# A trunk layer on one core: q, k and the probabilities of seven head pairs turned by VectorE's 32x32 transposes and a trip through DRAM, the normalization on ScalarE

## The chip, the cores and the metric

The kernel runs on one NeuronCore of a Trainium2 chip. A core has five engines with instruction streams of their own: TensorE (PE; its weight loads are a row of their own, PEld), VectorE (DVE), ScalarE (ACT), GpSimd (POOL) and SyncE (SP), which here does nothing but issue DMAs. Each engine works through its own instructions in the order in which the program lists them and stops at an instruction whose input is not there yet. Data moves between DRAM and the on-chip memory SBUF by DMA, over 16 engines that all queues share. The metric is the device time of one execution in microseconds (us), the median of several runs.

## What is computed

One layer of a diffusion backbone on 128 context tokens and 256 latent tokens with 2048 channels: modulation of the inputs, RMS norm, one input projection into q, k, v (16 heads of 64) and a Fourier branch, attention, gates, output projection, then a SwiGLU network. What the change touches is the attention, cut here to its core:

```
q = rms_norm(q.reshape(shp), q_g)
k = rms_norm(k.reshape(shp), k_g)
...
s_loc = jnp.einsum('brnqhd,brnkhd->bhrnqk', qg, kb).astype(jnp.float32) * scale + bias
s_ctx = jnp.einsum('brnqhd,blhd->bhrnql', qg, k_ctx).astype(jnp.float32) * scale
p = jax.nn.softmax(jnp.concatenate([s_loc, s_ctx], axis=-1), axis=-1).astype(v.dtype)
o = (jnp.einsum('bhrnqk,brnkhd->brnqhd', p[..., :nk], vb)
     + jnp.einsum('bhrnql,blhd->brnqhd', p[..., nk:], v_ctx))
```

Context tokens attend to context tokens only; latent tokens to a window of latent tokens and to the 128 cached context keys. `rms_norm` divides by the root of the mean square and multiplies by a gain. All in float32; the large products are made from three passes over halves of split operands (high times high, low times high, high times low).

## The kernel before

**Stages.** In order: the opening (modulation, first products), the input projection `w_in` (`unit`, from L163, with accumulation into SBUF at L783), the gate projection `w_gate` (the loop over `fc8`, 8 output chunks of 8 weight units), the branch projections `w_fn` and `w_na`, the output projection, the feed-forward part. TensorE's weights always come in units of 512 KB: `load_unit` (L230) issues the load on SP's queue, `split` (L155 on ACT, L156 on DVE) makes the high half `wh` and the low half `wl`, and `unit` multiplies: L170 and L171 with `wh`, L176 with `wl`, 18 products for two rows of weights and the three token tiles.

**Ticks.** The order of the work beside the products is written out by hand. `next_unit` (L249) and `mid_unit` (L245) call the generators in the lists `front` and `behind`; in the gate stage the list `front` holds the branch work (`br_work`: first the Fourier branch, then attention) and the row sums (`rows`), and each of the 64 units ticks them three times: at its start, after the split of a coming unit, and in its middle. So a tick of the gate stage is a third of a unit. `RATES[1]` = 0.62 is how many steps `rows` makes per tick there.

**Row sums.** `mod_rows` (L363 on DVE) multiplies 512 KB tiles of modulation weights by a scalar and adds them up, one instruction of 128x1024 per step; `CHUNKS` gives its steps per unit in the last pass of `w_in`, chunk by chunk in the order 6, 7, 0, 1, 2, 3, 4, 5, and `RATES[2]` in the branch projections. Its result is later added up across partitions by DMAs of the POOL queue. In the last pass of `w_in` a chunk takes five units.

**After a chunk of q or k.** `after` (L734) writes the chunk to DRAM (`s_qkvu`), squares it on ACT, sums per head and takes the inverse root on DVE; for k it also multiplies (L756) before it writes.

**Attention, one head pair at a time.** `attention_pair` (L946) goes through the ticks of the string `PAIR`, separated by commas; two letters name a step, a digit the half (0: the first 128 latent queries and the context queries, 1: the other 128 latent queries):

```
PAIR = "t1 qk,,,,,lq,s0 s1 m0,e0,m1,i0 pv lb,e1,,i1 t0,,lv"
```

`lq`, `lb`, `lv` issue the loads of the next pair (q and k, bias, v). `qk` (`turned`, L956) turns q and k, 128x128 blocks at a time, on TensorE against an identity (L960, L963: six transposes a pair) and copies them out of PSUM with ACT, which applies the gains (L965, L967, L968). `s` makes scores (L977, evicted at L989 to L998 into `sc`, 128 x 2 x 896), `m` the row maxima (L1004, L1008), `e` the exponentials with their sums (L1016, ACT), `i` the reciprocal (L1024) and the multiplication by it (L1026, both DVE: two 128x384 and, for half 0, two 128x128 as well). `t` (`keys_first`, L1028) turns the probabilities on TensorE (L1039: eight 128x128 blocks for half 0, six for half 1) and ACT copies them from PSUM into `pt` (L1041). `pv` multiplies by v (L1056) and evicts (L1060). `t1` and `pv` of a pair run in the ticks of the next one (`rest`); those of the last pair run after the loop.

The kernel already turns two other tensors with VectorE and DRAM, in `mixed` and in `turn_act`: L1142 or L1421 transposes every 32x32 block on DVE, L1146 or L1354 writes the tile to DRAM, and four DMAs (L1149 or L1358) read it back, 32 partitions each, so that the blocks come to their places.

Of the kernel before, what the change touches and what calls it, by code (L numbers as in the profile page):

```python
# [13 lines left out]
F32 = mybir.dt.float32  # L14
F32R = mybir.dt.float32r
AF = mybir.ActivationFunctionType
# [3 lines left out]
P = 128  # L20
# [7 lines left out]
CTX = 128  # L28
# [91 lines left out]
def trunk_kernel(ctx: ExitStack, tc: tile.TileContext, io: dict):  # L120
# [29 lines left out]
    def nm(s):  # L150
        return f"{s}{next(ids)}"
# [134 lines left out]
    s_sum = dram.tile([P, 4 * CH], F32, tag="sum", name="s_sum")  # L286
    s_turn = dram.tile([P, 4, TOK], F32, tag="turn", name="s_turn")

    first = consts.tile([P, 96], F32, tag="first", name="first")
# [17 lines left out]
    with ExitStack() as ph:  # L307
# [6 lines left out]
        def at_tile():  # L314
            return pa.tile([P, CH], F32, tag="at", name=nm("at"))
# [151 lines left out]
        with ExitStack() as pha:  # L467
# [266 lines left out]
            def after(ci):  # L734
                a = acc[ci]
                yield
                if not 2 <= ci < 4:
                    nc.sync.dma_start(s_qkvu[ci], a)
                if 4 <= ci < 6:
                    nc.sync.dma_start(new_v[:, (ci - 4) * CH : (ci - 3) * CH], a[:, 0])  # L740
                if ci >= 4:
                    return
                sq = c6([P, NT, CH], "sq")
                nc.scalar.activation(out=sq, in_=a, func=AF.Square)
                yield
                ss = small.tile([P, NT, 8], F32, tag="ssqk", name=nm("ssqk"))
                nc.vector.tensor_reduce(
                    out=ss, in_=sq.rearrange("p t (h d) -> p t h d", d=HD), axis=AX.X, op=ALU.add
                )
                if ci < 2:  # L750
                    yield from inv_sqrt(rq[:, :, ci * 8 : (ci + 1) * 8], ss, HD, [P, NT, 8])
                else:
# [5 lines left out]
                    nc.sync.dma_start(s_qkvu[ci], a)  # L758
# [147 lines left out]
        def attention():  # L906
            br = ph.enter_context(tc.tile_pool(name="branch", bufs=1))
            for i in range(8):
                aT[i] = br.tile([P, TOK], F32, tag=f"aT{i}", name=f"aT{i}")
            with ExitStack() as st:  # L910
                wk = st.enter_context(tc.tile_pool(name="awk", bufs=1))
                rest = {}
                for hp in range(8):
                    rest = yield from attention_pair(hp, wk, rest)
                rest["t1"]()
                for _ in range(5):
                    yield
                rest["pv"]()
# [5 lines left out]
        def load_qk(hp):  # L924
            ci, co = hp // 4, (hp % 4) * P
            qp = ald.tile([P, NT, P], F32, tag="qp", name=nm("qp"))
            kp = ald.tile([P, 4, P], F32, tag="kp", name=nm("kp"))
# [3 lines left out]
            return qp, kp  # L931

# [13 lines left out]
        def attention_pair(hp, wk, rest):  # L946
            (_, (qp, kp)), (_, bp), (_, vp) = qks[0].take(), biases[0].take(), vs[0].take()
            t = {}
# [7 lines left out]
            def turned():  # L956

                pq = at_tile()
                for i in range(NT):
                    nc.tensor.transpose(pq[:, i * P : (i + 1) * P], qp[:, i], ident)  # L960
                pk = at_tile()
                for i in range(NT):
                    nc.tensor.transpose(pk[:, i * P : (i + 1) * P], kp[:, i], ident)  # L963
                q = t["q"] = wk.tile([P, TOK], F32, tag="q", name=nm("q"))
                nc.scalar.activation(out=q, in_=pq[:, :TOK], func=AF.Identity, scale=qg8)  # L965
                k = t["k"] = wk.tile([P, 4 * P], F32, tag="k", name=nm("k"))
                nc.scalar.activation(out=k[:, :TOK], in_=pk[:, :TOK], func=AF.Identity, scale=qg[:, 1:2])  # L967
                nc.scalar.copy(k[:, TOK:], kp[:, 3])  # L968

# [51 lines left out]
            def inverses(qt):  # L1021
                sm = t["sm", qt]
                n = len(halves[qt])
                nc.vector.reciprocal(sm[:, :n], sm[:, :n])  # L1024
                for i, (j, sl) in enumerate(halves[qt]):
                    nc.vector.tensor_scalar_mul(sc[:, j, sl], sc[:, j, sl], sm[:, i : i + 1])  # L1026

            def keys_first(qt):  # L1028

                if not qt:  # L1030
                    t["pt"] = wk.tile([P, 16, P], F32, tag="pt", name=nm("pt"))
                blocks = [(j, qt * TOK + kc * P) for kc in range(3) for j in range(2)]
                if not qt:
                    blocks += [(j, 2 * TOK) for j in range(2)]
                for b0 in range(0, len(blocks), 4):
                    some = blocks[b0 : b0 + 4]
                    o = at_tile()
                    for i, (j, c0) in enumerate(some):
                        nc.tensor.transpose(o[:, i * P : (i + 1) * P], sc[:, j, c0 : c0 + P], ident)  # L1039
                    dst = slice(8 * qt + b0, 8 * qt + b0 + len(some))  # L1040
                    nc.scalar.copy(  # L1041
                        t["pt"][:, dst], o[:, : len(some) * P].rearrange("p (b q) -> p b q", q=P)
                    )

            def values():
# [3 lines left out]
                for k in range(4):  # L1049
                    for j in range(2):  # L1050
                        s = slice(j * HD, (j + 1) * HD)
                        out, x = po[s, :CTX], pt[:, 6 + j]
                        if k:
                            out = po[s, CTX:TOK].rearrange("p (t q) -> p t q", t=2)
                            x = pt.rearrange("p (t b) q -> p t b q", t=2)[:, :, 2 * k - 2 + j]
                        nc.tensor.matmul(  # L1056
# [8 lines left out]
                **{f"{n}{j}": functools.partial(f, j) for j in range(2) for n, f in (  # L1065
                    ("s", scores), ("m", maxima), ("e", exps), ("i", inverses), ("t", keys_first))},

                **{n: rest.get(n, lambda: None) for n in ("t1", "pv")},
            }
            for tick in PAIR.split(","):  # L1070
# [5 lines left out]
                yield  # L1076
            return {"t1": functools.partial(keys_first, 1), "pv": values}

# [546 lines left out]
```

## Time and profile before

| what | value |
|---|---|
| median of 3 runs | 2006.34 us (2005.43 to 2008.59) |
| the profiled execution: time | 2005.29 us |
| the profiled execution: span of the instructions | 2003.5 us |
| granted TensorE clock | 1.00 |
| attention's work on the engines | about 412 to 647 us from the span's start |

The page of the profile gives, for each engine, the time in which it ran an instruction ("busy") and its share of the span. The chain of work that ended last is found by going back from the last instruction to whatever released it; engines on that chain set the end, the others have room. A group line gives the line of the kernel, engine, operation, the names written and read, the shapes, the count, then busy time in us and the mean duration of one in ns, then the idle time just ahead of these instructions and what ended it. The view of stretches gives busy time per engine inside chosen bounds, the granted clock, the mean busy share of the 16 DMA engines and GB/s. TensorE's instructions are pipelined: one lasts longer than the distance to the next, so what one costs on the path is read from the chain, not from its duration.

### The profile page before, as it was taken

How to read it: one execution, taken by the hardware profiler on the slowest of the kernel's cores; microseconds unless marked ns; L12 is line 12 of the kernel's file. 1: busy time of each engine (PE TensorE's matmuls, PEld its weight loads, DVE VectorE, ACT ScalarE, POOL GpSimd, SP SyncE). 2: the span in 40 equal slices, each digit the busy share in tenths (PEclk: the TensorE clock that was granted, in tenths of full speed). 3: DMA queues.
4: the chain of work that ended last, by engine and by line, in shares of the span. 5: the costliest groups of instructions: out<-in, count | busy, mean ns of one | idle time of the engine just before them, and what ended most of it. 6: DMA issues, size and time to landing. Idle time of an engine off the chain costs nothing.

```text
span 2003.5 us, 24190 instructions
## 1 busy us (share of the span) xinstructions
PE 1989.5 (99%) x9404; PEld 1628.4 (81%) x9404; DVE 1226.0 (61%) x1493; ACT 718.3 (36%) x1052; POOL 73.9 (4%) x106
## 2 busy tenths in 40 slices
PE   8999999999999999999999999999999999999999
PEld 5767888887777888889988888888888888888887
DVE  6745999879877886776843454554334433434654
ACT  6324332445554443344423322323232233223231
POOL 0000010101010100100001000001000000000000
PEclk9999999999999999999999999999999999999999
DMA  9896898888886898764457464547444544455463
GB/s 347 289 342 206 308 288 312 271 278 283 269 255 216 284 330 264 252 231 131 134 182 200 158 189 164 188 139 211 137 150 129 165 153 131 132 152 174 158 185 104
DMA packets 140658, 425.28 MB, mean 212 GB/s; under 512 B 17856, under 2 KB 39296, under 8 KB 139520
## 3 DMA queue, kind: packets, MB, share of 16 engines
q1 hardware_dynamic: 127344, 400.51, 60.4%
q0 software_dynamic: 9600, 16.88, 3.9%
q10 hardware_dynamic: 3600, 6.34, 0.9%
q8 instruction: 74, 1.21, 0.2%
q14 instruction: 40, 0.33, 0.0%
HBM read 387.50 MB, written 44.63 MB: 216 GB/s over the span
## 4 chain that ended last, share of the span: by engine, by line
PE 95%; DMA 2%; DVE 2%; ACT 1%; issue 1%; SPq 0%; DVEq 0%; ACTq 0%
PE mm L170 19%; PE mm L176 18%; PE mm L171 18%; PE at L170 10%; PE at L171 10%; PE at L176 10%; PE at L436 1%; DMA wm<-in_w_mod 1%; PE at L1039 1%; PE at L977 1%; PE at L1056 1%; DVE wl L156 1%; PE at L1447 1%; PE at L1453 1%; PE mm L1453 1%; PE mm L1447 1%
## 5 line engine op out<-in xcount | busy, mean ns | idle before, releaser
L156 DVE TENSOR_TENSOR wl<-wraw,wh 128x1024 fp32r<-128x1024 f32 (+1 forms) x464 | 553.7, 1202 | 435.1 <-ACT wh L155 251.7
L155 ACT CAST wh<-wraw 128x1024 fp32r<-128x1024 f32 (+1 forms) x464 | 478.5, 1038 | 757.9 <-PE mm L171 454.1
L170 PE MATMUL mm<-wh,hH 128*128 128x512 f32 x1316 | 518.2, 394 | 0.3 <-ACT hH L155 0.3
L171 PE MATMUL mm<-wh,hL 128*128 128x512 f32 x1316 | 513.2, 390 | 0.2
L176 PE MATMUL mm<-wl,hH 128*128 128x512 f32 x1316 | 357.2, 389 | 0.2 <-DVE wl L156 0.2
L363 DVE SCALAR_TENSOR_TENSOR accr<-wmr,csz,accr 128x1024 f32<-128x1024 f32 x240 | 301.6, 1278 | 4.6 <-DMA wmr<-in_w_rows 4.6
L170 PEld LDWEIGHTS mm<-wh,hH 128*128 128x128 f32 x1316 | 247.0, 188 | 65.6 <-issue 12.7
L176 PEld LDWEIGHTS mm<-wl,hH 128*128 128x128 f32 x1316 | 246.9, 188 | 52.2 <-DVE wl L156 0.6
L171 PEld LDWEIGHTS mm<-wh,hL 128*128 128x128 f32 x1316 | 247.2, 188 | 50.6 <-DVE hL L156 0.8
L170 PE MATMUL at<-wh,hH 128*128 128x512 f32 x616 | 240.1, 390 | 0.0
L171 PE MATMUL at<-wh,hL 128*128 128x512 f32 x616 | 239.7, 389 | 0.0
L176 PE MATMUL at<-wl,hH 128*128 128x512 f32 x616 | 169.4, 389 | 0.0
L176 PEld LDWEIGHTS at<-wl,hH 128*128 128x128 f32 x616 | 115.6, 188 | 24.0
L171 PEld LDWEIGHTS at<-wh,hL 128*128 128x128 f32 x616 | 115.7, 188 | 23.9
L170 PEld LDWEIGHTS at<-wh,hH 128*128 128x128 f32 x616 | 115.6, 188 | 23.9
L170 PE MATMUL mm<-wh,cH 128*128 128x512 f32 x278 | 108.1, 389 | 0.0
L171 PE MATMUL mm<-wh,cL 128*128 128x512 f32 x278 | 108.1, 389 | 0.0
L176 PE MATMUL mm<-wl,cH 128*128 128x512 f32 x278 | 76.6, 389 | 0.0
L170 PE MATMUL at<-wh,cH 128*128 128x512 f32 x196 | 76.2, 389 | 0.0
L171 PE MATMUL at<-wh,cL 128*128 128x512 f32 x196 | 76.2, 389 | 0.0
L783 DVE TENSOR_TENSOR acc<-acc,mm 128x512 f32<-128x512 f32 x60 | 40.4, 685 | 43.8 <-PE mm L176 43.8
L171 PEld LDWEIGHTS mm<-wh,cL 128*128 128x128 f32 x278 | 52.2, 188 | 10.8
(287 smaller groups left out, 1817.1 us busy)
## 6 DMA issues: line engine op xcount, KB each, us to landing
wraw<-in_w_gate_up SPq DMA_DIRECT2D x176, 512.0 KB, 3.8
wmr<-in_w_rows SPq DMA_DIRECT2D x128, 512.0 KB, 5.2
wraw<-in_w_down SPq DMA_DIRECT2D x88, 512.0 KB, 3.9
wraw<-in_w_gate SPq DMA_DIRECT2D x64, 512.0 KB, 5.0
wraw<-in_w_in SPq DMA_DIRECT2D x60, 512.0 KB, 5.6
wm<-in_w_mod SPq DMA_DIRECT2D x24, 768.0 KB, 6.1
wraw<-in_w_o SPq DMA_DIRECT2D x32, 512.0 KB, 6.2
wm<-in_w_mod SPq DMA_DIRECT2D x28, 512.0 KB, 6.1
```

The source lines that it names most:

```text
L155: nc.scalar.copy(H, x)
L156: nc.vector.tensor_sub(L, x, fr(H))
L170: nc.tensor.matmul(po[t], H[k0 + i][:, sl], wH[:, i], start=first and i == 0, stop=False)
L171: nc.tensor.matmul(po[t], L[k0 + i][:, sl], wH[:, i], start=False, stop=False)
L176: nc.tensor.matmul(po[t], H[k0 + i][:, sl], wL[:, i], start=False, stop=last and i == n - 1)
L363: nc.vector.scalar_tensor_tensor(out=acc[:, cnd], in0=wm, scalar=sc, in1=acc[:, cnd], op0=ALU.mult, op1=ALU.add)
L436: nc.tensor.matmul(pm[q : q + 32, :w], csz[:, k, :], wm[:, kk + par, ty, :], start=k < 2, stop=k >= KT - 2, tile_position=(0, q), skip_gro ...
L783: nc.vector.tensor_add(a, a, po[t])
L977: nc.tensor.matmul(po[j][:, cols], t["q"][rows[j], q], t["k"][rows[j], k], start=True, stop=True, tile_position=(j * HD, 0),)
L1039: nc.tensor.transpose(o[:, i * P : (i + 1) * P], sc[:, j, c0 : c0 + P], ident)
L1447: nc.tensor.matmul(o, a, xH, start=u + kk == 0, stop=False)
L1453: nc.tensor.matmul(o, a, wide(u + kk)[0], start=False, stop=last and kk == 1)
```

## The change

q and k are no longer turned per pair on TensorE. `after` transposes the 32x32 blocks of every chunk of q and k on DVE once, three instructions of 128x512 per chunk (12 in all), and writes the result to new DRAM tiles `s_qk`; the old writes of these four chunks to `s_qkvu` go. `load_qk` reads q and k of a pair from there in four DMAs each, 32 partitions at a time; `turned` is left with three ACT instructions that read SBUF. The new `normed` multiplies the probabilities by their reciprocal sums on ACT instead of DVE, for all eight pairs. For pairs 0 to 6, `block_rows` transposes the 32x32 blocks of `sc` on DVE, `leave` writes them to DRAM (`s_pt`), and `enter` reads them back in four DMAs per half; pair 7 keeps TensorE's transposes. `pt` has a new layout (part, block, 32) that the products read in runs of 32 numbers. `PAIR` puts the new steps in its 15 ticks; `pv` moves two ticks later. The rows' steps per unit in chunks 1, 2, 3 and 4 go down by 0.35 (five units each) and those in the 32 units of the branch projections up by 0.22.

```diff
-PAIR = "t1 qk,,,,,lq,s0 s1 m0,e0,m1,i0 pv lb,e1,,i1 t0,,lv"
+PAIR = "x1 qk,w1,,,r0,lq,s0 s1 m0 r1,e0,m1,v0 lb,n0 e1,v1 pv,n1 x0,w0,lv"
-CHUNKS = [1.95, 1.95, 1.95, 1.6, 1.6, 1.2, 1.2, 1.7]
-RATES = [1.5, 0.62, 1.1, 1.3, 0.452]
+CHUNKS = [1.95, 1.95, 1.95, 1.25, 1.25, 0.85, 0.85, 1.7]
+RATES = [1.5, 0.62, 1.32, 1.3, 0.452]
...
-                if not 2 <= ci < 4:
+                if ci >= 4:
                     nc.sync.dma_start(s_qkvu[ci], a)
...
+                def channels_first():
+                    tr = c6([P, NT, CH], "sq").rearrange("p t n -> p (t n)")
+                    trv = tr.rearrange("p (g k t r) -> p k g t r", g=4, k=4, t=NT)
+                    for t in range(NT):
+                        nc.vector.transpose(
+                            trv[:, :, :, t], a[:, t].rearrange("p (k g r) -> p k g r", k=4, g=4)
+                        )
+                        if t < NT - 1:
+                            yield
+                    yield
+                    nc.sync.dma_start(s_qk[ci], tr.rearrange("p (g k n) -> p g k n", g=4, k=4))
...
-            nc.sync.dma_start(qp, s_qkvu[ci][:, :, co : co + P])
-            nc.sync.dma_start(kp[:, 0:3], s_qkvu[2 + ci][:, :, co : co + P])
-            nc.sync.dma_start(kp[:, 3], io["cache_k"][hp])
+            for x, src in ((qp, s_qk[ci]), (kp, s_qk[2 + ci])):
+                for g in range(4):
+                    nc.sync.dma_start(
+                        x[32 * g : 32 * g + 32], src[:, g, k].rearrange("(a p) n -> p a n", p=32)
+                    )
+            nc.sync.dma_start(kc, io["cache_k"][hp])
...
-                    nc.vector.tensor_scalar_mul(sc[:, j, sl], sc[:, j, sl], sm[:, i : i + 1])
+                    nc.scalar.activation(out=sc[:, j, sl], in_=sc[:, j, sl], func=AF.Copy, scale=sm[:, i : i + 1])
+
+            def block_rows(qt):
+
+                n = 6 if qt else 8
+                tr = t["tr", qt] = wk.tile([P, 4 * 8 * 32], F32, tag="tr", bufs=2, name=nm("ptr"))
+                b = tr[:, : 4 * n * 32].rearrange("p (g b r) -> p b g r", g=4, b=n)
+                for j in range(2):
+                    nc.vector.transpose(
+                        b[:, j:6:2],
+                        sc[:, j, qt * TOK : (qt + 1) * TOK].rearrange("p (c g r) -> p c g r", c=3, g=4),
+                    )
+                if not qt:
+                    nc.vector.transpose(b[:, 6:8], sc[:, :, 2 * TOK :].rearrange("p j (g r) -> p j g r", g=4))
+
+            def leave(qt):
+                n = 6 if qt else 8
+                nc.sync.dma_start(s_pt[qt], t["tr", qt][:, : 4 * n * 32].rearrange("p (g n) -> p g n", g=4))
...
+            def enter(qt):
+
+                if not qt:
+                    new_pt()
+                dst = t["pt"][:, :, 8:] if qt else t["pt"][:, :, :8]
+                for g in range(4):
+                    nc.sync.dma_start(
+                        dst[32 * g : 32 * g + 32].rearrange("p a b r -> p a (b r)"),
+                        s_pt[qt][:, g].rearrange("(a p) n -> p a n", p=32),
+                    )
```

In `PAIR`, `x` is `block_rows` (for pair 7 `keys_first`), `w` is `leave`, `r` is `enter`, `v` the reciprocal and `n` is `normed`; `x1`, `w1`, `r0`, `r1` and `pv` run in the ticks of the next pair.

More of the change, by code (lines that the diff above doesn't have):

```diff
@@ L287, in trunk_kernel @@
     s_turn = dram.tile([P, 4, TOK], F32, tag="turn", name="s_turn")
+    s_pt = [dram.tile([P, 4, n * 32], F32, tag=f"pt{n}", name=f"s_pt{n}") for n in (8, 6)]
+    s_qk = [dram.tile([P, 4, 4, NT * 32], F32, tag=f"sqk{i}", name=f"s_qk{i}") for i in range(4)]
     first = consts.tile([P, 96], F32, tag="first", name="first")
@@ L751, in after @@
                     yield from inv_sqrt(rq[:, :, ci * 8 : (ci + 1) * 8], ss, HD, [P, NT, 8])
+                    yield
+                    yield from channels_first()
                 else:
@@ L757, in after @@
                     yield
-                    nc.sync.dma_start(s_qkvu[ci], a)
+                    yield from channels_first()
                     nk = tmp.tile([P, 8, HD], F32, tag="junk", bufs=1, name=nm("nk"))
@@ L946, in attention_pair @@
         def attention_pair(hp, wk, rest):
-            (_, (qp, kp)), (_, bp), (_, vp) = qks[0].take(), biases[0].take(), vs[0].take()
+            (_, (qp, kp, kc)), (_, bp), (_, vp) = qks[0].take(), biases[0].take(), vs[0].take()
             t = {}
@@ L956, in turned @@
             def turned():
[L958 to L963, printed above, removed]
                 q = t["q"] = wk.tile([P, TOK], F32, tag="q", name=nm("q"))
-                nc.scalar.activation(out=q, in_=pq[:, :TOK], func=AF.Identity, scale=qg8)
                 k = t["k"] = wk.tile([P, 4 * P], F32, tag="k", name=nm("k"))
-                nc.scalar.activation(out=k[:, :TOK], in_=pk[:, :TOK], func=AF.Identity, scale=qg[:, 1:2])
-                nc.scalar.copy(k[:, TOK:], kp[:, 3])
+                for x, raw, g in ((q, qp, qg8), (k[:, :TOK], kp, qg[:, 1:2])):
+                    nc.scalar.activation(
+                        out=x.rearrange("p (t a r) -> p t a r", t=NT, a=4), in_=raw, func=AF.Identity, scale=g
+                    )
+                nc.scalar.copy(k[:, TOK:], kc)
             def scores(qt):
@@ L1041, in keys_first @@
                     nc.scalar.copy(
-                        t["pt"][:, dst], o[:, : len(some) * P].rearrange("p (b q) -> p b q", q=P)
+                        t["pt"][:, :, dst].rearrange("p a b r -> p b a r"),
+                        o[:, : len(some) * P].rearrange("p (b a r) -> p b a r", a=4, r=32),
                     )
@@ L1051, in values @@
                         s = slice(j * HD, (j + 1) * HD)
-                        out, x = po[s, :CTX], pt[:, 6 + j]
+                        out, x = po[s, :CTX].rearrange("p (a r) -> p a r", a=4), pt[:, :, 6 + j]
                         if k:
-                            out = po[s, CTX:TOK].rearrange("p (t q) -> p t q", t=2)
-                            x = pt.rearrange("p (t b) q -> p t b q", t=2)[:, :, 2 * k - 2 + j]
+                            out = po[s, CTX:TOK].rearrange("p (t a r) -> p t a r", t=2, a=4)
+                            x = pt[:, :, 2 * k - 2 + j :: 8].rearrange("p a t r -> p t a r")
                         nc.tensor.matmul(
@@ L1065, in attention_pair @@
                 **{f"{n}{j}": functools.partial(f, j) for j in range(2) for n, f in (
-                    ("s", scores), ("m", maxima), ("e", exps), ("i", inverses), ("t", keys_first))},
-                **{n: rest.get(n, lambda: None) for n in ("t1", "pv")},
+                    ("s", scores), ("m", maxima), ("e", exps), ("v", inverses), ("n", normed))},
+                "x0": functools.partial(keys_first if hp == 7 else block_rows, 0),
+                "w0": functools.partial(leave, 0) if hp < 7 else lambda: None,
+                **{n: rest.get(n, lambda: None) for n in ("x1", "w1", "r0", "r1", "pv")},
             }
@@ L1076, in attention_pair @@
                 yield
-            return {"t1": functools.partial(keys_first, 1), "pv": values}
+            if hp == 7:
+                return {"x1": functools.partial(keys_first, 1), "pv": values}
+            return {
+                "x1": functools.partial(block_rows, 1), "w1": functools.partial(leave, 1),
+                "r0": functools.partial(enter, 0), "r1": functools.partial(enter, 1), "pv": values,
+            }
         pha = ph.enter_context(ExitStack())
```

17 lines of the change are left out of this document (11 added, 6 removed).

## The prediction

> **What bounds the kernel now.** I read the page first: busy time, then the chain of work that ended last.
>
> ```profile
> PE 1989.5 (99%) x9404; PEld 1628.4 (81%) x9404; DVE 1226.0 (61%) x1493; ACT 718.3 (36%) x1052; POOL 73.9 (4%) x106
> ...
> PE 95%; DMA 2%; DVE 2%; ACT 1%; issue 1%; SPq 0%; DVEq 0%; ACTq 0%
> ```
>
> TensorE is on 95% of the chain. Work taken off it shortens the kernel, if nothing else steps into the place. Who could, is read stage by stage, from stretches: the last pass of `w_in` (213 to 340), the gate stage with the branches beside it (345 to 655), the branch projections (660 to 800), and two short ones inside the last.
>
> ```profile
> core 0: us, PE busy (x) PEld busy (x) DVE busy (x) ACT busy (x) POOL busy (x), PEclk, DMA share, GB/s
> 213.00:340.00 127.00, 127.00 (x562) 105.21 (x561) 121.85 (x133) 40.08 (x44) 9.26 (x12) 1.00 0.91 302
> 345.00:655.00 310.00, 308.49 (x1569) 247.24 (x1569) 245.72 (x322) 152.98 (x320) 29.11 (x40) 1.00 0.83 262
> ...
> 660.00:800.00 140.00, 140.00 (x619) 115.97 (x618) 113.55 (x129) 51.60 (x56) 10.35 (x14) 1.00 0.84 290
> ...
> 660.00:680.00 20.00, 20.00 (x90) 16.56 (x89) 17.25 (x19) 9.23 (x10) 2.35 (x3) 1.00 1.04 391
> ...
> 735.00:750.00 15.00, 15.00 (x68) 12.39 (x67) 13.14 (x16) 8.21 (x10) 0.00 (x0) 1.00 1.02 410
> ```
>
> TensorE never rests in any of them for more than 1.5 us, at a full clock. VectorE is second: 96% busy in the first, 79% in the gate stage, 81% after it. The DMA engines carry 262 GB/s there at a share of 0.83; that they can carry 410 at a share of 1.02 is seen later.
>
> What a transpose costs TensorE on the path is in the chain of pair 2 (start, length, what), and beside it the two places where TensorE stood still for one:
>
> ```profile
> 494.36 0.87 PE at L1039 x8
> 495.24 0.23 PE mm L170
> ...
> 499.34 0.66 PE at L1039 x6
> 499.99 0.33 PE at L960 x3
> 500.32 0.33 PE at L963 x3
> ...
> 436.00 1.22 PE at L1039 x8
> ...
> 463.40 1.22 PE at L1039 x8
> ...
> L1039 PE MATMUL at<-ident,sc 128*128 128x128 f32 x112 | 15.2, 273 | 1.3 <-DVE sc L1026 1.3
> ...
> L960 PE MATMUL at<-ident,qp 128*128 128x128 f32 x24 | 3.9, 273 | 0.0
> L963 PE MATMUL at<-ident,kp 128*128 128x128 f32 x24 | 3.9, 272 | 0.0
> ```
>
> One lasts 273 ns but the next begins 0.11 us later: eight take 0.87, six 0.66, three 0.33. The distance is what counts.
>
> **The change on TensorE.** q and k: 8 pairs x 2 x 0.33 = 5.3 us go. Probabilities: 7 pairs x (0.87 + 0.66) = 10.7 us go; pair 7 keeps its own. Sum 16.0. The stalls at 436 and 463 also go: 1.3 us idle and twice 0.35 us of the longer first run, 2.0 in all. But VectorE was late there by itself, and what TensorE needs next from it is the low half `wl` of the coming weights; I take half, 1.0. Nothing is added on TensorE. The products with v (L1056) now read `pt` in runs of 32 numbers, and no row has that shape on TensorE. If reading stayed as fast: 0; if it doubled a group of 1.66 us (below): 7 x 1.66 = 11.6. I take 0, since the Fourier products already read and write views of several parts at the pace of plain ones.
>
> ```profile
> 488.39 1.66 PE at L1056 x16
> ...
> 508.86 1.71 PE at L977 x12
> ```
>
> The *Trainium skill* speaks against the direction: *VectorE: DVE Perf Modes*, Rules for kernel authors, gives a full 128x128 transpose to TensorE, and The three transpose paths puts one at 390 ns there (bf16) against 311 ns for VectorE's 32x32 blocks. By 390 ns the 146 removed would be worth 57 us, by the trace's distance 16; I go by the trace, and TensorE being the bound is why the rule doesn't settle it here.
>
> **The change on VectorE and ScalarE.** These rows price the added and the removed:
>
> ```profile
> L1421 DVE STREAM_TRANSPOSE tr<-sg 128x512 f32<-128x512 f32 x30 | 21.4, 712 | 1.0
> ...
> L1026 DVE TENSOR_SCALAR sc<-sc,sm 128x384 f32<-128x384 f32 x32 | 12.0, 417 | 0.6
> ...
> L1026 DVE TENSOR_SCALAR sc<-sc,sm 128x128 f32<-128x128 f32 x16 | 3.8, 283 | 0.0
> ...
> L1041 ACT COPY pt<-at 128x512 f32<-128x512 f32 x24 | 13.3, 588 | 27.5 <-PE at L1039 27.5
> ...
> L1041 ACT COPY pt<-at 128x256 f32<-128x256 f32 x8 | 3.0, 378 | 0.0
> ...
> L1016 ACT ACTIVATE sc<-sc,mx 128x384 f32<-128x384 f32 x32 | 19.4, 610 | 2.9 <-DVE mx L1004 2.9
> ...
> L1016 ACT ACTIVATE sc<-sc,mx 128x128 f32<-128x128 f32 x16 | 6.2, 387 | 0.0
> ...
> L363 DVE SCALAR_TENSOR_TENSOR accr<-wmr,csz,accr 128x1024 f32<-128x1024 f32 x90 | 112.3, 1277 | 3.5 <-DMA wmr<-in_w_rows 3.5
> ...
> L156 DVE TENSOR_TENSOR wl<-wraw,wh 128x1024 fp32r<-128x1024 f32 x60 | 73.1, 1220 | 30.6 <-ACT wh L155 30.6
> ```
>
> Gate stage, VectorE: a 128x384 transpose, by its share of 712 ns, is an estimated 0.53 us, a 128x256 one 0.36; a pair gets 4 x 0.53 + 0.36 = 2.5 us (bounds 2.5 by size, 3.6 if each cost the full 712). It loses 4 x 0.417 + 2 x 0.283 = 2.2. So 7 x 0.3 minus pair 7's 2.2: nothing net (up to +7 us by the upper bound). VectorE's 246 us then lie in about 293 instead of 310: 84%.
> ScalarE: `normed` adds 4 x 0.61 + 2 x 0.39 = 3.2 us at most (by L1016, which also sums); 7 x (3 x 0.588 + 0.378) = 15.0 us of copies go, 8 x 3.2 = 25.8 come: 164 us in 293, 56%. Harmless as a sum.
>
> What changes is the order. `n0 e1` stand in one tick and VectorE's `v1` in the next, so VectorE waits for ScalarE to do n0 and e1: 2 x 0.61 + 2 x 0.39 + 2 x 0.61 = 3.2 us, less a tick of 4.08/3 = 1.36: up to 1.9 us a pair, 15 in all, with `wl` queued behind it. VectorE has 64 us idle in the stage, 30.6 of them only because ScalarE waits for TensorE to free `wh`; 17 go with the shorter stage. So these 15 fit, and `x0` behind `n0`, two ticks later, does too.
>
> `w_in`: 12 x 0.712 = 8.5 us come; the rows lose 4 chunks x 5 units x 0.35 = 7 steps x 1.277 = 8.9 us. Nothing net, chunk by chunk 2.1 against 2.2, but at 96% busy a late transpose could cost: 0 to 3.4 us (8.5 less the 5.15 idle), I take 0.5. SP holds the write of `s_qk` until the third transpose is done, with weight loads queued behind it; before, the writes of k waited for L756 in the same way.
> Branch projections: 32 x 0.22 = 7 steps, 9.0 us, on 113.55 of 140: 88%. 0 to 3 us, I take 0.5.
>
> **The change on SP and the DMA engines.** Per pair `sc` is 128 x 7168 bytes = 0.92 MB; it is written and read: 1.84 MB more, 12.8 MB for seven pairs. q and k keep their bytes.
>
> ```profile
> q1 hardware_dynamic: 127344, 400.51, 60.4%
> ...
> q10 hardware_dynamic: 3600, 6.34, 0.9%
> ...
> s_turn<-tr SPq DMA_DIRECT2D x10, 768.0 KB, 3.5
> ...
> turned<-s_turn SPq DMA_DIRECT2D x40, 192.0 KB, 5.0
> ...
> SPq L230 <- DVE wl L156: 105.8, 38, 9.0
> SPq L340 <- DVE accr L363: 67.4, 31, 7.9
> ...
> ACT wh L155 <- DMA wraw<-in_w_gate: 1.8, 1, 1.8
> ...
> L1358 SPq DMA_DIRECT2D turned<-s_turn x40: 319/426/434, 1060.1 to 1906.7; - x40
> ```
>
> By bytes (queue q10: 0.9% of 2003.5 us for 6.34 MB, 2.84 us of all 16 engines per MB) a pair adds 5.2 us; by packets (256 to write, 1024 to read, 256 more for q and k) 7.7 at q10's 80 ns each and 14.6 at q1's 152. I take 6, since q10's packets are the nearest in size. 0.83 x 310 = 257 us of DMA time become 257 + 42 = 299 in 293 us: a share of 1.02, at (81 + 13 MB)/293 = 321 GB/s. That looks full, but the same share carried 410 GB/s for 15 us, and the loads wait for buffers, not for data: SP waits 173 us in this stage for VectorE to free one, and ScalarE met a late gate weight once, for 1.8 us. A few late loads: 0 to 17 us, I take 2.5.
> SP issues 8 + 2 + 6 DMAs more per pair, at 0.43 us: 6.8 us of about 24, out of its waiting.
>
> The way back of half 1: `w1` waits for `x1` with loads behind it, `r1` (5 ticks later) for `w1`'s landing, `pv` (5 ticks later) for `r1`. `r1` to `pv` are 5 x 1.36 + 1.71 (the scores, L977) = 8.5 us; four issues and one landing need 1.7 + 5.0 = 6.7. 1.8 us to spare; I take 0.
>
> The *Trainium skill*, *DMA: Bandwidth & Descriptors*, Specifications, asks for at least 512 bytes a run for full rate; q and k now come in runs of 384. By that they would cost more per byte; no row here isolates such a run.
>
> **Sum.** 2005.3 - 16.0 - 1.0 + 0.5 + 0.5 + 2.5 = 1991.8 against the profiled execution. The median lies 1.05 us above it: 1992.8, said as 1992.5.
>
> **The rivals.** *VectorE and ScalarE wait for each other.* If the 15 us of waits at `v1` don't fit, since each comes in one piece ahead of a `wl` that TensorE needs, about half reaches TensorE: 1992.5 + 7.5 = 2000. For: VectorE's stop before 436 did reach it. Against: it was a single one, in a stretch crowded with Fourier work.
> *The probabilities come late.* Landings above the median, or a `w1` late behind VectorE, make TensorE wait at `pv` about 1.5 us in each of seven pairs: 10.5, so 2003, no change that counts. For: only 1.8 us to spare and fuller DMA engines. Against: half 0 has a tick more.
> *The DMA engines fill up, and it gets slower.* If the average share cannot pass 1.05, the stage lasts longer than now from (1.05 x 310 - 257)/7 = 9.8 us of added DMA time per pair; at 12, between the two packet prices, (257 + 84)/1.05 = 325 us, +15: 2021. For: packets of 0.4 to 1 KB, and 0.91 is the highest share held over 100 us here. Against: the 410 GB/s, and q10's packets.
>
> **How the numbers follow.** Forecast 1992.5 (its own range 1987 to 1998): 62%; waits of VectorE and ScalarE, 2000: 16%; late probabilities, 2003: 10%; full DMA engines, 2021: 12%. The low end is the sum without new stalls and with all 2.0 of the old ones, 1988, less 2 for the runs' spread: 1986; the high end takes in the first two rivals: 2004. Within 0.2%, about what a measurement here can tell from no change, is 2002.3 to 2010.4. Faster: 62 + 16 = 78%; same: 10%; slower: 12%.
>
> **What would show it.** Right: no TensorE rows that read `qp` or `kp`, and 14 transposes of `sc` instead of 112; TensorE still 99% busy; the gate stage 14 to 17 us shorter, the others unchanged. Waits of TensorE for `wl` in mid pair, with VectorE waiting for `sc`'s exponentials, are the first rival; TensorE waiting for a DMA into `pt`, the second; waits for `wraw` and `wmr`, with a DMA share above 1 across the stage, the third. A longer L1056 group than 1.66 us would make the price of the new layout wrong; a stretch before 340 longer than now, the balance of `CHUNKS`.

## The result, and the profile after

| | before | after |
|---|---|---|
| median (lowest to highest), us | 2006.68 (2005.43 to 2011.36) | 2043.46 (2040.98 to 2047.36) |
| profiled execution, and its span, us | 2005.29, 2003.5 | 2041.82, 2040.0 |
| mean granted clock of TensorE | 1.0 | 0.991 |

The ratio is 1.0184, with an interval from 1.0172 to 1.0196. The kernel became slower by 37 us, outside the range that was forecast. The page of after first, its busy times and the engines' shares of the chain that ended last:

```profile
PE 1987.4 (97%) x9258; PEld 1619.0 (79%) x9258; DVE 1233.6 (60%) x1492; ACT 727.9 (36%) x1072; POOL 73.7 (4%) x106
PE 85%; DMA 6%; DVE 4%; ACT 2%; issue 1%; SPq 1%; ACTq 0%; DVEq 0%
```

The 146 transposes are gone from TensorE, and yet it is busy as long as before: what is left runs slower in places. On the chain, TensorE fell from 95% to 85%, and the DMAs went from 2% to 6%. Next TensorE's waits in after (us in all, times, longest):

```profile
PE at L1107 <- DMA pt<-s_pt: 34.7, 6, 9.0
PE at L513 <- DMA xc<-in_x_in: 3.9, 1, 3.9
PE at L438 <- DMA wm<-in_w_mod: 3.2, 5, 0.8
```

One wait stands out: the product with v (L1107) waits for the probabilities' way back from DRAM, after six of the seven pairs. The stretches tell where the time went (TensorE's busy time is the second number, then its instructions; at the end of a line granted clock, DMA share, GB/s). Before:

```profile
345.00:690.00 345.00, 343.49 (x1724) 276.22 (x1724) 275.56 (x357) 170.69 (x339) 34.82 (x48) 1.00 0.83 267
470.00:640.00 170.00, 170.00 (x875) 133.13 (x874) 139.86 (x183) 88.70 (x200) 15.51 (x22) 1.00 0.81 255
```

After:

```profile
213.00:340.00 127.00, 127.00 (x562) 105.13 (x562) 122.66 (x140) 40.64 (x44) 8.95 (x12) 1.00 0.86 288
345.00:690.00 345.00, 306.97 (x1432) 239.77 (x1431) 246.36 (x308) 162.51 (x342) 27.34 (x38) 0.95 0.87 272
470.00:640.00 170.00, 143.63 (x644) 107.71 (x641) 115.51 (x145) 79.39 (x178) 16.96 (x24) 0.90 0.92 282
660.00:800.00 140.00, 138.66 (x632) 112.68 (x631) 116.62 (x130) 59.91 (x76) 9.12 (x12) 1.00 0.84 285
```

Nearly the whole loss lies in the gate stage: the first write of `s_turn` behind it starts at 727.9 us in place of 692.8, 35.1 later, and the spans differ by 36.5. From 345 to 690 TensorE rests 38.0 us in place of 1.5, which is 36.5 more. The clock of 0.95 there stands for five stretches at 0.5, of 37.6 us together. Some 15 of these fall into the waits themselves and cost nothing more; in the other 22 TensorE works at half pace, which costs 11. With 16 saved that makes some 32 of the 35. The lower clock comes with the waits, as the chain of after shows around the third pair's return (start, length, what):

```profile
502.16 1.52 PE at L1107 x12
503.68 0.43 PE mm L170
504.11 0.23 PE mm L171
...
529.04 2.41 DMA pt<-s_pt
531.45 0.14 issue
531.59 2.83 PE at L1107 x12
534.42 0.73 PE mm L170
535.14 0.43 PE mm L171
535.57 0.43 PE mm L170
536.00 0.43 PE mm L171
536.42 0.79 PE mm L176 x2
537.21 0.23 PE mm L170
```

After a wait of 1.2 us (the pair at 502) twelve products take 1.52 us. After one of 4.1 us the same twelve take 2.83, and the matmuls behind them 0.43 each in place of 0.23, for some 5 us in all. The *Trainium skill*, *TensorE: Matmul & The Clock Gate*, Why this matters for your kernels, asks for no idle gaps of more than about 3 us between matmuls, since the clock falls back behind them; the trace agrees for these two waits. In other runs the edge isn't sharp: in e1 (below) waits of 2.8 and 2.9 us were each followed by 3.4 us at a clock of 0.5, and in e10 one of 3.2 us was not.

Why the probabilities were late shows in SP's own timeline of after (start, length of the issues, line, what):

```profile
514.90 0.33 SPq L1062 DMA_DIRECT2D s_pt<-ptr  x1
517.26 0.33 SPq L342 DMA_DIRECT2D wmr<-in_w_rows  x1
518.40 0.33 SPq L230 DMA_DIRECT2D wraw<-in_w_gate  x1
518.78 2.13 SPq L1073 DMA_DIRECT2D pt<-s_pt  x4
520.96 4.06 SPq L947 DMA_DIRECT2D qp<-s_qk  x4
525.15 1.95 SPq L947 DMA_DIRECT2D kp<-s_qk  x4
527.14 0.43 SPq L950 DMA_DIRECT2D kc<-in_cache_k  x1
527.62 1.85 SPq L1073 DMA_DIRECT2D pt<-s_pt  x4
```

TensorE began the scores of the tick that holds `r1` at 516.1 and reached the product at 526.1. SP issued `r1` at 527.6: it stood five ticks of `PAIR` behind TensorE's place in the program, held by weight loads that wait for VectorE, then by nine q/k loads. Those take long to issue because of what SP waits for in 400 to 650:

```profile
SPq L947 <- DMA wraw<-in_w_gate: 10.2, 7, 2.3
SPq L947 <- DMA wmr<-in_w_rows: 9.5, 6, 3.6
SPq L947 <- DMA pt<-s_pt: 9.3, 12, 3.1
```

The q/k loads use none of this data. In the trace's semaphore events the DMAs of SP and ScalarE raise eight completion semaphores in turn, and a DMA isn't issued until the one eight places before it has landed. So at most eight are in flight in these runs (whether the chip or the program's build sets that number, no run here shows), and SP issues 26 to 34 a pair where it was 14 to 18 before.

### The profile page after: what moved, and what is told of

Read it like the earlier page. It is cut to its first block, busy times and chain, and to the rows that moved or that the text cites. A ratio compares the mean times of both kernels' runs of the same rounds, so it can differ in the third digit from the quotient of the medians.

```text
span 2040.0 us, 24070 instructions
## 1 busy us (share of the span) xinstructions
PE 1987.4 (97%) x9258; PEld 1619.0 (79%) x9258; DVE 1233.6 (60%) x1492; ACT 727.9 (36%) x1072; POOL 73.7 (4%) x106
## 4 chain that ended last, share of the span: by engine, by line
PE 85%; DMA 6%; DVE 4%; ACT 2%; issue 1%; SPq 1%; ACTq 0%; DVEq 0%
PE mm L170 17%; PE mm L171 16%; PE mm L176 16%; PE at L176 9%; PE at L170 9%; PE at L171 9%; DVE accr L365 2%; DMA pt<-s_pt 1%; PE at L438 1%; DMA wm<-in_w_mod 1%; DMA wmr<-in_w_rows 1%; PE at L1107 1%; DVE wl L156 1%; DMA gl<-s_turn 1%; DMA s_gate<-gst 1%
```

## The experiments

Two theories. By the first, the queue (S or Q in the expectations), the loss is one of order and count: what must be early stands behind what needn't be, in one queue. By the second, the DMA engines (D or B), the 12.8 MB more are what costs, in whatever order. All times are medians, each beside runs of the kernel before on the same chip (2005.4 to 2006.5 us there).

| run | us | ratio to before, with interval |
|---|---|---|
| e1_lq_behind | 2031.83 | 1.0132 [1.0107, 1.0156] |
| e12_slack | 2041.87 | 1.0182 [1.0167, 1.0197] |
| e9_order_and_slack | 2042.74 | 1.0185 [1.017, 1.0201] |
| e7_fewer_dmas | 2040.68 | 1.017 [1.0146, 1.0194] |
| e2_p_alone | 2040.22 | 1.017 [1.0155, 1.0185] |
| e10_p_slack_cols | 2019.0 | 1.0063 [1.0048, 1.0078] |
| e4_bytes_beside | 2043.72 | 1.0187 [1.0166, 1.0207] |
| e5_bytes_clean | 2035.44 | 1.0141 [1.0125, 1.0158] |
| e6_quarter_bytes | 2019.7 | 1.0061 [1.0041, 1.0081] |
| e16_order_quarter | 2018.41 | 1.0065 [1.0048, 1.0082] |
| e13_p_quarter | 2002.44 | 0.9986 [0.9977, 0.9996] |
| e15_every_other | 2010.8 | 1.0031 [1.0018, 1.0045] |
| e14_qk_on_pool | 2059.45 | 1.0271 [1.0256, 1.0287] |
| e18_fewer_order | 2035.22 | 1.0147 [1.0133, 1.0161] |
| e11_all | 2049.8 | 1.0217 [1.02, 1.0234] |
| e3_qk_alone | 2007.6 | 1.0008 [0.9999, 1.0018] |
| e8_qk_rows_later | 2022.93 | 1.008 [1.0061, 1.0098] |
| e17_qk_paced | 2013.18 | 1.0039 [1.0025, 1.0053] |

### Order and slack, with the whole change

The first run puts the q/k loads behind `r1`:

```diff
-PAIR = "x1 qk,w1,,,r0,lq,s0 s1 m0 r1,e0,m1,v0 lb,n0 e1,v1 pv,n1 x0,w0,lv"
+PAIR = "x1 qk,w1,,,r0,,s0 s1 m0 r1 lq,e0,m1,v0 lb,n0 e1,v1 pv,n1 x0,w0,lv"
```

> Edit: in PAIR the loads of the next pair's q and k (lq, nine DMAs) stand behind r1 instead of ahead of it; nothing else. Theory S (SP's queue: the eight DMAs of r0 and r1 and the nine of lq are issued one after another, each also waiting for the landing of the DMA eight places before it, so r1 goes out some 10 us after TensorE's scores): r1 goes out 5 to 8 us earlier, TensorE's waits for pt fall from 34.7 us to under 12, the clock in the gate stage comes back to 0.97 or more, time 1992 to 2015. Rival D (the 16 DMA engines are full with the 12.8 MB more): the same bytes in the same ticks, so the waits for pt stay at 25 us or more and the time at 2030 to 2050.

The order is worth 11 us: less than the queue theory said, and the waits for `pt` fall to 15.0 us, further than the engine theory said. TensorE's largest waits of this run:

```profile
PE at L1107 <- DMA pt<-s_pt: 15.0, 8, 2.9
PE mm L176 <- DVE wl L156: 6.6, 4, 3.5
```

The return is still late, though no q/k load stands between `r0` and `r1` now, and a second wait, for the low half of weights, has come up. So the product was also moved, first alone, then with the order:

```diff
-PAIR = "...r0,lq,s0 s1 m0 r1,e0,m1,v0 lb,n0 e1,v1 pv,n1 x0,w0,lv"
+PAIR = "...r0,lq,s0 s1 m0 r1,e0,m1,v0 lb,n0 e1,v1,n1 x0,w0,pv lv"      # e12
+PAIR = "...r0,,s0 s1 m0 r1 lq,e0,m1,v0 lb,n0 e1,v1,n1 x0,w0,pv lv"     # e9
```

> The change with the values' product three ticks later and nothing else. If slack alone is what was missing, stalls fall from 10.3, 1.4, 6.5, 7.3, 7.8, 9.1 to 6, 0, 2.4, 3.2, 3.7, 5 us and the time by about 21 us plus half of the lost clock: 2010 to 2025. If the queue's order is the cause and slack is eaten by the same queue (it runs behind TensorE's place and is held by landings), the stalls stay over 5 us each: 2030 to 2043.

> The change with the q/k loads put behind the return of half 1 and the values' product three ticks (about 4.1 us) later, just ahead of the next value load. If the loss is only that the probabilities' way back is longer than the ticks leave it, the stalls that were left with the loads behind (3.7, 1.7, 3.6, 5.0, 1.9, 6.8, 0 us) lose 4.1 each: about 4 us of waits for pt in the gate stage in place of 34.7, clock in 470:640 at 0.97 or more, time 1998 to 2012. If the DMA engines' load is what costs (everything that is loaded comes late, whatever the order), the waits move to weight loads and columns and the time stays at 2020 to 2035.

Alone it does nothing (waits for `pt` still 25.5 us, longest 9.6): the queue eats the slack. With both, the wait for `pt` is gone altogether, and the time is that of the change. TensorE's two largest waits in e9, and VectorE's largest in 400 to 700:

```profile
PE mm L176 <- DVE wl L156: 16.3, 7, 6.0
PE at L993 <- ACT sc L1014: 7.9, 1, 7.9
```

```profile
DVE accr L365 <- DMA wmr<-in_w_rows: 37.3, 10, 9.4
```

VectorE stands still for a late row weight (`wmr`), with `wl` behind it in its order, and TensorE waits for `wl`. The queue theory in its simple form falls here: the late return was the first wait to show, and when it is taken away, other waits take its place (TensorE's rest from 345 to 690 is 30.7 us in e9, 38.0 in after). Why e9 is 11 us above e1 was not settled.

Fewer DMAs for the same bytes, in the change's own order (both halves out in one DMA and back in four; q/k loads for two pairs at a time):

```diff
-                for g in range(4):
-                    nc.sync.dma_start(x[32 * g : 32 * g + 32], src[:, g, k].rearrange("(a p) n -> p a n", p=32))
+            if k % 2 == 0:
+                    for g in range(4):
+                        nc.sync.dma_start(..., src[:, g, k : k + 2].rearrange("(a p) k n -> p a (k n)", p=32))
...
+                if qt:
+                    nc.sync.dma_start(s_pt, t["tr"].rearrange("p g b r -> p g (b r)"))
```

> Edit: the change with the same bytes in fewer DMAs: both halves of the probabilities leave in one DMA (in w1) and come back in four (in r1) instead of eight, and q and k are loaded for two pairs at a time, eight DMAs every second pair instead of every pair. lq stays ahead of r1. Per pair some 25 SP DMAs instead of 34. Theory S: waits for pt fall below 15 us and the clock comes back, time 1995 to 2022. Rival D: the same bytes, and all of them now come back in the last five ticks, so waits for pt stay at 30 us or more, time above 2035.

TensorE still waits 27.1 us for `pt`: 20.0 of them in the three pairs where the q/k loads precede the return, 7.1 in two others.

### The bytes

First the probabilities alone: `PAIR`, `normed`, `block_rows`, `leave` and `enter` as in the change; `load_qk`, `turned` and the two lists as before:

```diff
-CHUNKS = [1.95, 1.95, 1.95, 1.25, 1.25, 0.85, 0.85, 1.7]
-RATES = [1.5, 0.62, 1.32, 1.3, 0.452]
+CHUNKS = [1.95, 1.95, 1.95, 1.6, 1.6, 1.2, 1.2, 1.7]
+RATES = [1.5, 0.62, 1.1, 1.3, 0.452]
```

> Edit: only the probabilities take the trip through DRAM, with PAIR as in the change; q and k are loaded in two DMAs and turned on TensorE as before, CHUNKS and RATES as before. Theory S: lq is three DMAs instead of nine, r1 goes out about 4 us earlier: waits for pt under 15 us, time 1998 to 2020. Rival D: q and k are the same bytes either way, so nearly the full loss stays: 2025 to 2045.

The probabilities alone lose 34.6 us: 20.0 us of waits for `pt`, and one of 10.9 for `colr`, the columns of the row sums. Then the same with these two waits taken away:

```diff
-PAIR = "...r0,lq,s0 s1 m0 r1,e0,m1,v0 lb,n0 e1,v1 pv,n1 x0,w0,lv"
+PAIR = "...r0,,s0 s1 m0 r1 lq,e0,m1,v0 lb,n0 e1,v1,n1 x0,w0,pv lv"
-                after = {3: (4, 16), 5: (3, 9)}
+                after = {3: (4, 24), 5: (3, 9)}
```

> Only the probabilities' part (q and k turned on TensorE as before), with the q/k loads behind the return of half 1, the values' product three ticks later, and the columns of modulation type 4 asked for after 24 in place of 16 steps of the rows. If the lateness of the return and one early demand for columns are the whole loss of the probabilities alone (20 us of waits for pt and 10.9 for colr in that run), the part keeps its 10.7 us: 1994 to 2004. If bytes cost time by themselves, 2015 to 2030 as with bytes beside the kernel before.

21 us come back. The stretch of this run:

```profile
470.00:640.00 170.00, 155.48 (x741) 116.97 (x738) 134.41 (x168) 87.76 (x202) 15.54 (x22) 0.98 0.97 309
```

No wait is put down to `pt` or `colr` any more, and 13.3 us of loss remain although 10.7 are saved: 24 us have no single place. From 345 to 690 TensorE rests 19.0 us in place of 1.5, most of it in small waits for halves of weights (the rows are of the whole run):

```profile
PE mm L170 <- ACT wh L155: 9.6, 7, 3.8
PE mm L176 <- DVE wl L156: 5.9, 7, 1.5
```

The DMA engines run at a share of 0.97 over 170 us. So the bytes were added to the kernel before, without the change, on GpSimd's queue, at the ticks of the change:

```diff
-PAIR = "t1 qk,,,,,lq,s0 s1 m0,e0,m1,i0 pv lb,e1,,i1 t0,,lv"
+PAIR = "t1 qk,w1,,,r0,lq,s0 s1 m0 r1,e0,m1,i0 pv lb,e1,,i1 t0,w0,lv"
...
+            nc.gpsimd.dma_start(s_out[2 * hp + qt], xtra[0]...)
...
+                nc.gpsimd.dma_start(xtra[1 + qt][32 * g : 32 * g + 32, :, : n * 32], s_in[:, g, : n * 32]...)
```

> Edit: the kernel before, with the change's trips of the probabilities (same shapes and runs, same ticks, about 13 MB) added as extra traffic from a tile of zeros on GpSimd's queue, which nothing waits for; no other change. Theory S: the DMA engines take it, TensorE stays above 99% busy in the gate stage, time 2004 to 2012. Rival D: as many bytes on the same 16 engines make loads late, time above 2020.

> Edit: the kernel before, with the same 12.8 MB in the same runs and ticks as the change, on GpSimd's queue, now from and to tiles of their own so that no extra transfer waits for another one (in the earlier run they did, and held up the row sums of the same queue). Nothing waits for them. Theory S (SP's queue: small DMAs in series, at most eight from SP and ScalarE in flight): the bytes alone cost TensorE nothing, time 2004 to 2012. Rival D (the 16 DMA engines are full): weights or row tiles late all through the gate stage, time above 2018.

In e4 the added DMAs held up the row sums in GpSimd's queue, and two waits (18.8 us for `colr`, 15.7 behind a VectorE that waited for the sums) make its loss: it tells nothing. In e5, without waits between the added DMAs, the loss is 28.9 us, but 14.0 of it is again `colr` and 5.8 one `wh`. The loss is of the size expected of the bytes, its place is not. So the bytes were taken away with the DMAs kept, a quarter of bytes and packets each: in the change's order, with the probabilities alone, and with the whole change mended. All three leave three quarters of `pt` unfilled (it is one tile, zeroed once), so they leave out that part of the product.

```diff
-                nc.sync.dma_start(s_pt[qt], t["tr", qt][:, : 4 * n * 32]...)
+                nc.sync.dma_start(s_pt[qt][:32], t["tr", qt][:32, : 4 * n * 32]...)
...
-                        dst[32 * g : 32 * g + 32].rearrange(...),
-                        s_pt[qt][:, g].rearrange(...),
+                        dst[32 * g : 32 * g + 32, :1].rearrange(...),
+                        s_pt[qt][:32, g].rearrange(...),
```

> Edit: the change with the same 70 DMAs for the probabilities in the same order and ticks, each carrying a quarter of the bytes (32 of 128 partitions leave, 32 rows of each part come back; the other three quarters of pt stay zero, so this part of the product is left out). Theory S: count and order are the same, each landing a little shorter: TensorE's waits for pt stay above 20 us, time 2022 to 2042. Rival D: 9.6 MB of 12.8 are gone, waits for pt under 8 us, time below 2005.

> The probabilities alone with order, slack and columns mended (2019.0 us), the same DMAs, but each moves a quarter of its bytes; three quarters of pt are left as they were. The kernel before moves 255 GB/s x 170 us = 43.4 MB in 470:640, the trips of seven pairs add 7 x 1.835 = 12.8 MB, and the mended kernel reached 309 GB/s at a DMA share of 0.97, so 318 full: 56.2 MB need 177 us where TensorE would need 170 - 14 = 156. Theory B (the DMA engines are full): with 46.6 MB, 147 us, there is room again: 1993 to 2000, clock over 0.99. Theory Q (SP's one queue, its many DMAs and the eight in flight): 2012 to 2020, as the count is unchanged.

> The whole change with the loads behind and the product three ticks later (2042.7 us), same DMAs, a quarter of the bytes of the probabilities' trips. Theory B (engines full, order no longer the matter): 1995 to 2010, against 2019.7 for the same bytes in the change's own order. Theory Q (queue): 2020 to 2040 with the late row weights (VectorE's wait for wmr, 37.3 us) still there.

Three pairs of runs, with losses against before: 36.8 becomes 13.2 (the change and e6), 37.0 becomes 13.0 (e9 and e16), 13.3 becomes -3.0 (e10 and e13). Three quarters of 12.8 MB, 9.6 MB, are worth 24, 24 and 16 us: 1.7 to 2.5 us per MB, in each order. This is shown, and for the change it is the larger part of the loss. In each pair the waits that were there shrink: those for `pt` from 34.7 to 15.4 us (the change and e6), VectorE's for `wmr` from 37.3 to 16.4 (e9 and e16), and the two rows of e10 above become, in e13:

```profile
PE mm L170 <- ACT wh L155: 2.6, 5, 1.5
PE mm L176 <- DVE wl L156: 2.2, 2, 1.7
```

What these runs don't separate: packets fell together with the bytes, and a DMA that lands sooner also gives its place among the eight in flight back sooner. The landing of a gate weight (median us at the end of a row), in 470 to 640 of before, e13 and e10:

```profile
wraw<-in_w_gate SPq DMA_DIRECT2D x30, 512.0 KB, 4.6
```

```profile
wraw<-in_w_gate SPq DMA_DIRECT2D x30, 512.0 KB, 5.4
```

```profile
wraw<-in_w_gate SPq DMA_DIRECT2D x30, 512.0 KB, 6.9
```

These three rise with the DMA share (0.81, 0.87, 0.97), but the landing doesn't follow the share alone: in e9 it is 7.5 us at 0.89, in e15 (next) 5.4 at 0.91.

Is there a threshold, below which bytes are free? With trips for every other pair, and two buffers for `pt`, the stage moves 292 GB/s at a share of 0.91:

```diff
+TURNED = (1, 3, 5, 7)
...
-                "x0": functools.partial(keys_first if hp == 7 else block_rows, 0),
+                "x0": functools.partial(keys_first if hp in TURNED else block_rows, 0),
```

> The probabilities alone with order, slack and columns mended, but only head pairs 0, 2, 4 and 6 go through DRAM; 1, 3, 5 and 7 are turned on TensorE as before. q and k as before. TensorE saves 4 x 1.53 = 6.1 us; the stage moves 43.4 + 3.5 x 1.835 = 49.8 MB, which is 157 us at 318 GB/s, of some 165. Theory B: it fits, no waits over 2 us, 1996 to 2002, faster than the kernel before. Theory Q: each trip costs its own waits, about half of the 14 us lost in the mended kernel: 2008 to 2014.

It loses 5.4 us where 6.1 are saved: 11.5 us for 7.3 MB, 1.6 per MB at most. It did not beat the kernel before. Part of it is a wait of another kind (6.4 us in four pieces in the profiled execution, which took 2014.6 us: TensorE's transposes of the pairs that stayed, waiting for ScalarE's normalization), so how much of the 11.5 the bytes cost stays open; but the expectation of a gain once the bytes fit did not hold. With the probabilities alone, what was lost beside the saving is 7.7 us at 3.2 MB (e13), 11.5 at 7.3 and 24 at 12.8: it grows with the bytes, and it is there below a full share, too.

### The queue, with the bytes kept

With a quarter of the bytes the whole change still lies 16 us above the probabilities alone (losses of 13.0 and -3.0; beside q and k the two differ in the row rates and in when the columns are asked for). Two runs on this part. The first sends the nine q/k loads over GpSimd's queue:

```diff
-                    nc.sync.dma_start(
+                    nc.gpsimd.dma_start(
                         x[32 * g : 32 * g + 32], src[:, g, k].rearrange("(a p) n -> p a n", p=32)
```

> As the whole change with order and slack mended (2042.7 us), but the nine q/k loads of a pair go out on GpSimd's queue: the same bytes and runs, SP's DMAs per pair from about 34 to 25. Theory Q (SP's queue is what everything else waits in): 2005 to 2022, VectorE's wait for wmr falls from 37.3 to under 20. Theory B (engines full): 2030 to 2045, the waits move. A wait for the row sums' columns (colr), whose DMAs share GpSimd's queue, would be an accident of this form.

```profile
PE at L993 <- ACT k L984: 47.2, 2, 27.3
```

Its loss is two waits for q and k, whose loads stood behind the row sums' DMAs in GpSimd's order. VectorE's wait for `wmr` fell to 6.8 us, as the queue theory said; but a TensorE that stands still for 47 us also asks for less, so this doesn't prove it. The second has fewer DMAs (the edits of e7 together with those of e9):

> The whole change with order and slack mended (2042.7 us) and fewer DMAs for the same bytes: one out and four in for a pair's probabilities, q/k loads for two pairs at a time. SP's DMAs fall from about 34 to 25 a pair. If the count in one queue makes the second half of the loss (16 us between a quarter of the bytes with and without the q/k part, 2018.4 and 2002.4): 2020 to 2030, VectorE's wait for wmr under 20 us in place of 37.3. If bytes in short runs are the whole of it: 2038 to 2045.

7.5 us come back, and VectorE waits 22.4 us for `wmr`; a wait for `colr` of 10.0 us in this run is not in e9. Its q/k runs are twice as long too (768 bytes): packets under 512 bytes in 470 to 640 are 3134 in place of 8880. Whether count or run length did it, the run can't tell. All mends together, with the row steps put back into the gate stage (the edits of e9, the columns at 24, and the rates):

```diff
-RATES = [1.5, 0.62, 1.32, 1.3, 0.452]
+RATES = [1.5, 0.655, 1.1, 1.3, 0.452]
```

> The whole change with all three mends (loads behind, product three ticks later, columns at 24 steps) and the rates of the two stages of rows set so that the seven steps of the rows that moved to the branch projections go back into the gate stage (RATES[1] 0.655, RATES[2] 1.1). If lateness in queues is the whole loss, both savings are kept: 1988 to 2000. If the DMA engines' load costs by itself: 2015 to 2035. If the steps of the rows cannot be placed in either stage without being late (as with q and k alone at 1.1), 2003 to 2015 with a wait for colr in 800:1000 or a late gl in 690:740.

The slowest of these orders on SP's queue: TensorE waits 35.4 us for `wl`, and VectorE 48.5 for `wmr`. More row steps in the stage with the late row weights went with longer waits for them.

### q and k alone

The change without its probabilities (`PAIR`, `keys_first` and the normalization as before), and the same with other rates of row steps:

```diff
 RATES = [1.5, 0.62, 1.32, 1.3, 0.452]      # e3, as in the change
+RATES = [1.5, 0.62, 1.1, 1.6, 0.452]       # e8
+RATES = [1.5, 0.655, 1.1, 1.3, 0.452]      # e17
```

> Edit: only q and k are turned by VectorE and DRAM, with CHUNKS and RATES of the change; the probabilities and PAIR as before. Theory S: 17 fewer small DMAs wait in SP's queue than in the change and nobody on TensorE waits for one soon: 5 us less TensorE, time 1999 to 2006. Rival D: hardly any bytes more: also 1999 to 2006. Rival W (the balance of CHUNKS and RATES, or the 384-byte runs, is what costs): above 2012.

> Edit: q and k alone through VectorE and DRAM (as in e3), with the seven row steps that the change puts into the branch projections put into the output projection instead (RATES[2] 1.32 to 1.1, RATES[3] 1.3 to 1.6). Theory B (what ate the 5 us of e3 are TensorE's waits for weights between 700 and 745, where the row tiles make the way back of the gated tiles late): no such wait there, time 2000 to 2004. Rival: q and k cost it in the gate stage itself, time stays at 2006 to 2009.

> q and k alone (2007.6 us), with the steps of the rows that its shorter gate stage leaves over put back into the gate stage (RATES[1] 0.655) and the branch projections at the 1.1 of the kernel before. If the q/k part is good for the 5.3 us that the prediction gave it and lost them only to the seven steps of the rows that moved into the branch projections: 1999 to 2003, no wait for gl or wh over 2 us in 660:800. If the q/k loads in short runs cost by themselves, 2005 to 2010 with no single place that shows it.

None is faster than before. In e3 the gate stage runs without waits (TensorE busy 342.91 of 345 us, clock 1.00) and the first write of `s_turn` behind it starts 3.7 us earlier than before (689.08 and 692.78); but the branch projections give it back. Their stretch in e3, and the wait in it:

```profile
660.00:800.00 140.00, 134.48 (x582) 110.53 (x581) 116.30 (x133) 48.43 (x52) 12.26 (x16) 0.98 0.89 285
```

```profile
PE at L170 <- ACT wh L155: 5.5, 2, 4.0
```

The chain runs there through the turned gates (`gl<-s_turn`, 10.2 us in one piece), for which ScalarE waits with the cast of that `wh` behind it. In e8 that wait is 2.7 us, but one for `colr` of 16.6 follows after 800, since the rows are late there. In e17, with the row steps of before, two waits of 4.5 and 3.7 us stand in the same stretch. So it isn't only the seven row steps that moved; what makes the gates late there stays open.

## Why the prediction was wrong

- **The transposes leave TensorE, 16.0 us.** They left. The nearest to getting the gain is e13, which leaves out part of the product, with 3.0 of its 10.7; q and k got none of their 5.3 by the end of the kernel. The stalls at 436 and 463 (1.0 in the sum) went too, but two waits of 0.6 and 0.7 us for a `wh` came near 439 and 446: nothing was won there.
- **The new layout of `pt` at nothing.** Right. Before, and in e9, where no wait disturbs it (mean ns after the busy us):

```profile
L1056 PE MATMUL at<-pt,vp 128*64 128x256 f32 x96 | 11.7, 379 | 0.0
```

```profile
L1107 PE MATMUL at<-pt,vp 128*64 128x256 f32 x96 | 11.8, 380 | 0.2 <-issue 0.2
```

- **VectorE and ScalarE.** Right in size: transposes took 0.554 and 0.403 us (0.53 and 0.36 estimated), and VectorE's wait for ScalarE, "up to 1.9 us a pair, 15 in all", shows in 400 to 700 of after as

```profile
DVE sm L1040 <- ACT sc L1032: 13.0, 7, 1.9
```

and didn't reach TensorE there. The first rival didn't come.
- **`w_in` and the branch projections at 0.5 each.** `w_in` cost nothing (127.00 of 127 us), the projections 1.3 us of rest in after.
- **"The way back of half 1: 1.8 us to spare; I take 0".** Failed, and it is what the page shows first: 34.7 us. The sum placed `r1` at TensorE's tick. SP issued it 11.5 us later (527.6 against 516.1), although TensorE needed 10.0 us to the product and not 8.5, and the last landing took 2.4 and not 5.0; it was late since its queue ran behind and "out of its waiting" counted SP's issues but not their order, nor that only eight may be in flight. This was the second rival, priced at 1.5 us a pair; it came at up to 9.0. But e9 shows that this term alone wasn't the root: with it gone, the loss stayed.
- **"A few late loads: 0 to 17 us, I take 2.5".** The step that cost most. A share of 1.02 was worked out and waved through, because 410 GB/s had been seen for 15 us. From 470 to 640 the highest that any run held was 0.97 and 309 GB/s, and the price was there below that: 1.7 to 2.5 us per MB, against the 0.2 per MB that 2.5 us for 12.8 MB mean. It is near the 2.84 us of engine time per MB that the prediction itself had from queue q10; whether that is more than chance, no run shows. The loads were late as the third rival said, but not by its rule: the share over 470 to 640 never passed 0.97. So it is partly luck that its 2021 lies near the 2019.0 of e10, where the bytes stand without the late returns.
- **Not in the sum:** the clock behind the waits, some 11 us of after.

Open: why the whole change costs 16 us more than the probabilities alone even with a quarter of the bytes (count in the queue, or short runs; a higher DMA share is not it, since e9 loses 37.0 us at a share of 0.89 and e10 13.3 at 0.97), and why the gates come late with q and k alone. No version that does the whole work was faster than the kernel before.

## What to carry to other kernels

Moving work from a full engine to the DMA engines can have a price per byte, even where their share reads 0.83: here a pair's transposes were worth 1.53 us on TensorE and its 1.84 MB cost 3 to 4.6 us (at 1.7 to 2.5 per MB), so work out what is saved per MB first (0.83 us here). A DMA's issue time is read from where its queue stands in the trace, not from the tick it is written at; count what precedes it. When a wait is removed and the time doesn't move, look for the next load that is late, and take bytes away with the order kept: that helps to tell a short resource from a bad order.

## What the hardware showed that was not expected

- In these traces SP and ScalarE share eight completion semaphores for their DMAs, so a q/k load of 48 KB stood for a weight load's landing (29.0 us of such waits in 400 to 650 of after, in the three rows above).
- TensorE ran at half pace for some 5 us behind a wait of 4.1 us, and at full pace behind one of 1.2; in e1 waits of 2.8 and 2.9 us already cost 3.4 us at a clock of 0.5.
- The median landing of the same 512 KB load went from 4.6 us at a DMA share of 0.81 over 5.4 at 0.87 to 6.9 at 0.97 with the probabilities alone; with q and k in short runs beside them (e9) it was 7.5 at 0.89.
